# A hybrid mixer's tokens in a new order: convolution inputs first, retention gates made movable

## The chip, the cores and the metric

The kernel runs on one core of one Trainium2 chip. The metric is the device time of one call, in microseconds. Before the change the median of 3 runs is 2538.73 us (2537.46 to 2539.43).

## What is computed

One inference step of two trunk layers over 640 tokens of width 1024 (128 context tokens, 512 latent ones). Each layer is feed-forward, mixer, feed-forward, each added to x. The change touches the mixer alone. It projects the normed x by `w_in` into twelve pieces and runs four parallel head groups of width 256, which `w_out` brings back:

```python
aq, ak, av, bq, bk, bv, cx, cy, dq, dk, dv, dg = split_columns(u)
# A: windowed attention, normed q and k, 2-D rotary, cached context keys, a sink logit
oa = window_attention(axial_rope(qa), axial_rope(ka), va, kca, vca, sink)
# B: dense attention over cached context plus all latent tokens
ob = dense_attention(axial_rope(qb), concat([kcb, axial_rope(kb)]), concat([vcb, vb]), None)
# C: width-4 convolution, gates, recurrence h = a*h + b both ways, GeLU branch
xc = centred_conv(cx, conv_w, conv_b)
r, i = sigmoid(xc @ wa + ba), sigmoid(xc @ wx + bx)
a = exp(-8 * r * softplus(-lam));  b = sqrt(1 - a*a) * i * xc
oc = (hf + hb) * gelu(cy)
# D: retention both ways, normed per head, swish gate
o = rms_norm_per_head(retention(dq, dk, dv)) * gain
od = silu(dg) * o
x = x + g2 * (concat([oa, ob, oc, od]) @ w_out)
```

The context tokens run the same formulas among themselves, and their keys, values and final states are outputs too.

## The kernel before, in words

The kernel works on x transposed: 8 tiles of 128 features by 640 tokens. A product in fp32 is made of three passes over a high and a low part (`mm3`, lines 274 to 276): high by high, high by low, low by high. Weights arrive from memory as `raw` (512 KB each) and are split on chip: ScalarE writes `whi` (L169), VectorE writes `wlo` (L170).

The mixer is cut into **tokens**. Each stream is a generator, and one letter of the string `ORDER` lets that generator issue its next piece. So the string sets the program order on every engine, and with it the order in which the weight loads, the slots of the tile rings and the PSUM banks are asked for. A scheduler then moves instructions of different tokens past each other by priority; `order` rows below are the result. The streams are:

- `C` the branch of the convolution and its gates (`conv`, `gates`, `gelu_in`, lines 874 to 927), `L` the recurrence (`lru`, from L931: products on GpSimd, scans on VectorE at L961 to L966).
- `a`, `b` the projections dq and dk of the two head pairs of retention (`dproj`, from L982), `v` its values in natural layout, `r`, `s` retention itself (`retention`, from L1032). In it `rs` is the score product, `pm` the score times the decay mask `tt` on VectorE (L1068), and `ro` the product with the values (L1074). The end of `retention` multiplies by the gain and by the gate `sg` (L1136, L1137).
- `p`, `q` the projections q, k, v of the two attentions (`qkv`, from L1144): two passes of five blocks each. A block is 24 matmuls of 128x256 into `nat` (L1026 to L1028), then a chain through VectorE and GpSimd: sum of squares (L1191, L1192), power -1/2 on GpSimd (L1194), scale (L1196), gain on GpSimd (L1198), rotary on both (L1210, L1213), add (L1215 or L1224).
- `t`, `u` the transposes of finished q and k blocks on TensorE (`tr`, L1165), copied out at L1168, L1169, L1173 and L1174. They need the add of their blocks.
- `m`, `n` the scores of the windowed and dense attention (L1271, L1272) with row maximum (L1297), exponential (L1306) and scale (L1313); `M`, `N` the transposes of the probabilities (`pt` L1323, copied to `PT` at L1324) and the products with the values (`ao` L1332); `c` halves of the down projection (`dn`).
- `|` changes the PSUM pools from 3 two-bank score tiles and 2 one-bank tiles to 2 and 4, and `!` loads the cached keys and values (`load_cache`, L1243).

All wide tiles (split weights, masks `tt`, probabilities `P` and `PT`, cached keys) share one ring of slots, so a load waits until its slot's last reader is done. ScalarE, VectorE and GpSimd each run their list strictly in order.

The mixer opens with `first(l, 1)`, which projects three column chunks of `w_in` straight after the norm. They are the first three in the packed weight `wint`.

Of the kernel before, what the change touches and what calls it, by code (L numbers as in the profile page):

```python
# [4 lines left out]
F32 = mybir.dt.float32  # L5
F32R = mybir.dt.float32r
BF = mybir.dt.bfloat16
AF = mybir.ActivationFunctionType
OP = mybir.AluOpType
AX = mybir.AxisListType.X  # L10

L = 2
T = 640
# [25 lines left out]
SUM1 = 1  # L39
BC1 = 4  # L40
ORDER = (
    "CaCCCCvLvrLarvvvLLLbsLvpLrprbrssrqsrsrLsptrsLpppqLp|spqtpqLsptqpqpqtq!mqmmqMmqMmMmqMmMmuMmcMmuMmMmcM"
    "mMmuMmcMmuMmMmcMmMmcMnMnMMncNnNncNnNncNnNncNnNncNnNnNncNnNncNnNncNnNnNNcNcNc",) * L


def segs(a, b):
# [8 lines left out]
def trunk(tc, A, O):  # L55
    nc = tc.nc
    V, S, G, PE, D = nc.vector, nc.scalar, nc.gpsimd, nc.tensor, nc.sync
    from contextlib import ExitStack, nullcontext
    with ExitStack() as es:
# [24 lines left out]
        def slot(name, dt=F32, w=SLOT):  # L84
            return wp.tile([128, w], dt, tag="w", name=name)
# [150 lines left out]
        def plan():  # L236
            for l in range(L):
                ffn_units(l, 0)
                own = {"C": {0: 3, 1: 4, 3: 5}, "a": {0: 6, 1: 7}, "b": {0: 8, 1: 9}}
                own = {t: {i: [(A["wint"][l, c], 1024)] for i, c in v.items()} for t, v in own.items()}  # L240
                own["v"] = {0: [(A["wdv"][l, h], 1024) for h in range(2)]}
                for t, m in (("p", 0), ("q", 1)):
                    own[t] = {6 * i: [(A["wqkv"][l, m, 2 * i + h], 1024) for h in range(2)] for i in range(2)}
                own["c"] = {4 * h: [(A["wocd"][l, h], 1024)] for h in range(4)}
                for c in range(3):
                    plain(A["wint"][l, c], 1024)
                done = {}
# [482 lines left out]
        C = {}  # L730

        def mixer_consts():
# [14 lines left out]
            used = [0]  # L747

            def tiny(name, w):
                if name in ("lru_n", "lru_p", "lg", "nlg", "kdec", "dgain8"):  # L750
                    return cp.tile([128, w], F32, name=name)
                used[0] += w
                return temps[:, used[0] - w:used[0]]
# [77 lines left out]
            G.tensor_tensor(kdec, ebase[:, :8 * L], kd_x, op=OP.pow)  # L831

            dgain = ccol[:, 38 * L:40 * L]
            dgain8 = tiny("dgain8", 2 * L)
            V.tensor_scalar(dgain8, dgain, 8.0, None, OP.mult)
            C.update(rcos=rcos, rsin=rsin, masks=masks, idb=idb, blk2=blk2, ccol=ccol, sink=sink, negsink=negsink, stc=stc, lru_n=lru_n, lru_p=lru_p, lg=lg, nlg=nlg, kdec=kdec, dgain8=dgain8)

        def mixers(l):
            rcos, rsin, masks, idb, blk2, ccol, sink, negsink, stc, lru_n, lru_p, lg, nlg, kdec, dgain8 = [C[n] for n in "rcos rsin masks idb blk2 ccol sink negsink stc lru_n lru_p lg nlg kdec dgain8".split()]
            cc = ccol  # L840
            CW = lambda j, c: cc[:, l * 10 + c * 5 + j:l * 10 + c * 5 + j + 1]
            o1 = 10 * L
# [3 lines left out]
            o3 = 18 * L  # L846
            H0 = lambda d, c: cc[:, o3 + l * 4 + d * 2 + c:o3 + l * 4 + d * 2 + c + 1]
            o4 = 22 * L
            DG = lambda c: dgain8[:, l * 2 + c:l * 2 + c + 1]
            SN = lambda d, c: lru_n[:, l * 4 + d * 2 + c:l * 4 + d * 2 + c + 1]  # L850
            SPc = lambda d, c: lru_p[:, l * 4 + d * 2 + c:l * 4 + d * 2 + c + 1]

# [5 lines left out]


            other()  # L860
            h, (v0, v1, vcx), _ = first(l, 1)
            sg = []
            for v in (v0, v1):
                t = slot("sg", F32, T)
                S.activation(t, v, AF.Silu)
                sg.append(t)

            def tchunk(name):
                u = take()
# [8 lines left out]
            def conv(v, c):  # L878
                xp = slot("xp")
                G.memset(xp[:, 0:2], 0.0)  # L880
                G.memset(xp[:, 130:133], 0.0)
                G.memset(xp[:, 645:646], 0.0)
                S.activation(xp[:, 2:130], v[:, 0:128], AF.Copy)
                S.activation(xp[:, 133:645], v[:, 128:640], AF.Copy)
                y = slot("y")
                V.tensor_scalar(y[:, :643], xp[:, 2:645], CW(2, c), CW(4, c), OP.mult, OP.add)
                for j in (0, 1, 3):
                    V.scalar_tensor_tensor(y[:, :643], xp[:, j:j + 643], CW(j, c), y[:, :643], OP.mult, OP.add)
                ys.append(y)

            conv(vcx, 0)
            act = {}

            def gates(c):
# [19 lines left out]
                G.tensor_mul(x2, x2, cy)  # L914
                return x2, cy

            cys, gts = [], []

            def branch():
                conv(tchunk("cx"), 1)  # L920
                yield
                for c in range(2):
                    cys.append(gelu_in(tchunk("cy")))
                    yield
                    gts.append(gates(c))
                    yield

            def behind(name):
# [324 lines left out]

            def attention(m):
                qs, ks, vn = att[m]
                cv = cache["v"]
                for g in range(2):
                    if (2 * m + g) not in mixed:
                        mixed[2 * m + g] = (slot("mxh", F32R, T), slot("mxl", F32R, T))
# [6 lines left out]
                def scores(b, g, kv):  # L1266
                    q2 = qs[g][kv][:, b * 128:b * 128 + 128]

                    def mm2(out, keys, c, last=True):

                        PE.matmul(out, q2, keys[0][:, c], start=True, stop=False)  # L1271
                        PE.matmul(out, q2, keys[1][:, c], start=False, stop=last)  # L1272

                    p = psS("sc")
                    if b == 0:
                        mm2(p[:, 512:640], ks[kv], slice(0, 128))
                        lo, hi = 512, 640
                        vs = [vn[:, 0:128]]
                    else:
                        n = b - 1  # L1280
                        mm2(p[:, 256:512], cache["k"][kv], slice(m * 256, m * 256 + 256))
                        n0, n1 = (max(0, n - 1), min(4, n + 2)) if m == 0 else (0, 4)
                        w = (n1 - n0) * 128
                        k0 = 128 + n0 * 128
                        band = [(n - 1, 0), (n + 1, 1)] if m == 0 else []
                        band = [(j, i) for j, i in band if n0 <= j < n1]
                        mm2(p[:, 512:512 + w], ks[kv], slice(k0, k0 + w), not band)
                        for e, (j, i) in enumerate(band):
                            c0 = 512 + (j - n0) * 128
                            PE.matmul(p[:, c0:c0 + 128], idb, masks[:, i * 128:i * 128 + 128], start=False,  # L1290
                                      stop=e == len(band) - 1)
                        lo, hi = 256, 512 + w
                        vs = [cv[:, m * 256 + i * 128:m * 256 + i * 128 + 128] for i in range(2)]
                        vs += [vn[:, 128 + j * 128:256 + j * 128] for j in range(n0, n1)]
                    w = hi - lo
                    mx = small("mx", 1)
                    V.tensor_reduce(mx, p[:, lo:hi], AX, OP.max)  # L1297
                    nm = small("nm", 1)
                    if m == 0:
                        si = l * 4 + g * 2 + kv  # L1300
                        V.tensor_scalar(nm, mx, -0.125, negsink[:, si:si + 1], OP.mult, OP.min)
# [12 lines left out]
                    return P, w, vs
# [51 lines left out]
            def att_step(m, i):  # L1366

                if m not in attm:
# [2 lines left out]

            mod_until((l, 5))
            g2 = modt[(l, 5)]
            streams = {"C": branch(), "L": lru(), "a": dproj(0), "b": dproj(1), "v": dvalues(),
                       "r": retention(0), "s": retention(1), "p": qkv(0), "q": qkv(1), "t": qktr(0), "u": qktr(1),
                       "m": att_step(0, 0), "M": att_step(0, 1), "n": att_step(1, 0), "N": att_step(1, 1),
                       "c": down(KC, 2, 4, mixed, (4, 5, 6, 7), g2, halves=True)}
# [45 lines left out]
def _layout(inp):  # L1423
    import numpy as np
    f = np.float32
    a = {}
# [23 lines left out]
    def dn(w):  # L1450
# [3 lines left out]
    w = g["w_in"]  # L1454
    cw = cols(w)
    base = {"cx": 8, "cy": 10, "dq": 12, "dk": 14, "dv": 16, "dg": 18}
    order = [base["dg"], base["dg"] + 1, base["cx"], base["cx"] + 1, base["cy"], base["cy"] + 1,
             base["dq"], base["dk"], base["dq"] + 1, base["dk"] + 1]
    a["wint"] = asc(cw[:, order])

    def nat(cols_, kper):
# [94 lines left out]
```

## Time and profile before

| what | value |
|---|---|
| median of 3 runs | 2538.73 us (2537.46 to 2539.43) |
| the profiled execution's own time | 2538.78 us |
| its span in the trace | 2537.0 us |
| granted TensorE clock, mean | 0.985 |
| TensorE busy | 2448.2 us, 96% of the span |
| VectorE, ScalarE, GpSimd busy | 1986.8 us (78%), 1149.7 us (45%), 238.8 us (9%) |
| instructions | 43717 |

The profiled execution's time exceeds its span by 1.8 us, and it is within 0.1 us of the median, so microseconds read in the span can be taken off the time one for one. The mixer of layer 0 fills about 507 to 844 us, that of layer 1 starts 1247.0 us later (1753.98 us against 506.96 us for the first copy out of the opening chunks) and fills 1754 to 2092 us. The rest of the span is feed-forward and norms, which the diff does not touch.

### The profile page before, as it was taken

To read this page: it belongs to the slowest core of one execution; us is meant where nothing else is said; L and a number is where in the kernel's file an instruction comes from. 1 tells how busy PE (TensorE), PEld (TensorE's weight loads), DVE (VectorE), ACT (ScalarE), POOL (GpSimd) and SP (SyncE) were. 2 spreads that over 40 slices of the span, in tenths; PEclk is the share of its full clock that TensorE was granted. 3 is DMA by queue.
4 is the path that set the end of the run, shared out by engine and by line. 5 is a ranking of instruction groups with operands and counts; after the bars stand their busy time and mean duration, and the time that the engine had idled before them with its cause. 6 is when DMAs were issued, how large, how long until landed. Compare 5 with 4: busy or idle time off the path is not lost. (4 is left out here: it accounts for less than half of the span.)

```text
span 2537.0 us, 43717 instructions
## 1 busy us (share of the span) xinstructions
PE 2448.2 (96%) x17252; PEld 2363.3 (93%) x17252; DVE 1986.8 (78%) x3876; ACT 1149.7 (45%) x2301; POOL 238.8 (9%) x251
## 2 busy tenths in 40 slices
PE   7999999998889999999999999999997899999999
PEld 6999999996778999999999999999786799999999
DVE  5899989856576798988989898897656768666765
ACT  5344343563355634443463344344523646333433
POOL 2100000032500200000020000000433002000000
PEclk9999999999989999999999999999998999999999
DMA  7544334222002244443424444332110022222222
GB/s 252 190 151 142 124 132 140 88 82 70 17 26 67 85 152 139 142 128 121 142 88 147 133 142 133 125 125 78 59 58 22 18 76 80 72 74 77 91 79 72
DMA packets 92653, 262.39 MB, mean 103 GB/s; under 512 B 10144, under 2 KB 21024, under 8 KB 92448
## 3 DMA queue, kind: packets, MB, share of 16 engines
q1 hardware_dynamic: 92448, 259.60, 31.4%
q8 instruction: 136, 2.23, 0.4%
q14 instruction: 69, 0.57, 0.1%
HBM read 256.15 MB, written 3.41 MB: 102 GB/s over the span
## 5 line engine op out<-in xcount | busy, mean ns | idle before, releaser
L274 PE MATMUL dn<-hidh,wp 128*128 128x320 f32 x1408 | 434.3, 311 | 0.1
L275 PE MATMUL dn<-hidl,wp 128*128 128x320 f32 x1408 | 433.7, 309 | 0.2 <-DVE hidl L282 0.2
L276 PE MATMUL dn<-hidh,wp 128*128 128x320 f32 x1408 | 433.3, 309 | 0.0
L169 ACT ACTIVATE wp<-ws 128x512 fp32r<-128x512 f32 x288 | 180.6, 630 | 391.7 <-DVE ws L216 151.0
L683 DVE SCALAR_TENSOR_TENSOR x<-dn,mod,x 128x128 f32<-128x128 f32 (+3 forms) x488 | 234.3, 520 | 137.6 <-PE dn L276 136.6
L169 ACT ACTIVATE wp<-raw 128x512 fp32r<-128x512 f32 (+1 forms) x408 | 243.5, 611 | 208.9 <-DVE wp L170 84.2
L319 DVE SCALAR_TENSOR_TENSOR junk<-wm,cond 128x1024 bf16<-128x1024 f32 x256 | 305.0, 1221 | 5.3 <-DMA wm<-in_wmod 4.9
L170 DVE TENSOR_TENSOR wp<-raw,wp 128x512 fp32r<-128x512 f32 (+1 forms) x408 | 266.2, 668 | 51.8 <-ACT wp L169 47.3
L274 PEld LDWEIGHTS dn<-hidh,wp 128*128 128x128 f32 x1408 | 264.0, 188 | 4.6 <-ACT hidh L281 3.7
L275 PEld LDWEIGHTS dn<-hidl,wp 128*128 128x128 f32 x1408 | 264.4, 188 | 0.6 <-DVE hidl L282 0.6
L276 PEld LDWEIGHTS dn<-hidh,wp 128*128 128x128 f32 x1408 | 264.4, 188 | 0.0
L170 DVE TENSOR_TENSOR wp<-ws,wp 128x512 fp32r<-128x512 f32 x288 | 197.9, 692 | 17.3 <-ACT wp L169 16.8
L275 PE MATMUL g<-hl,whi 128*128 128x320 f32 x608 | 192.4, 317 | 2.1 <-DVE hl L529 1.4
L274 PE MATMUL g<-hh,whi 128*128 128x320 f32 x608 | 185.9, 318 | 4.6 <-ACT hh L528 1.9
L276 PE MATMUL g<-hh,wlo 128*128 128x320 f32 x608 | 190.3, 314 | 0.0
L274 PE MATMUL x<-hh,wp 128*128 128x320 f32 x576 | 178.2, 309 | 0.8 <-DVE sl L614 0.8
L276 PE MATMUL x<-hh,wp 128*128 128x320 f32 x576 | 178.2, 309 | 0.0
L275 PE MATMUL x<-hl,wp 128*128 128x320 f32 x576 | 178.0, 309 | 0.0
L170 DVE TENSOR_TENSOR wlo<-raw,whi 128x1024 fp32r<-128x1024 f32 x88 | 110.4, 1256 | 64.6 <-ACT whi L169 49.3
L426 POOL TENSOR_TENSOR nrs<-nrm,neghalf 80x4 f32<-80x4 f32 x12 | 13.3, 1107 | 1432.5 <-DVE nrm L424 1432.5
L1026 PE MATMUL nat<-whi,hh 128*128 128x256 f32 x400 | 119.5, 299 | 9.2 <-ACT qsq L1187 5.8
L169 ACT ACTIVATE whi<-raw 128x1024 fp32r<-128x1024 f32 x88 | 92.6, 1052 | 66.3 <-DVE pmc L1092 13.7
(333 smaller groups left out, 6646.2 us busy)
## 6 DMA issues: line engine op xcount, KB each, us to landing
raw<-in_wgu SPq DMA_DIRECT2D x176, 512.0 KB, 3.5
wm<-in_wmod SPq DMA_DIRECT2D x128, 512.0 KB, 3.6
raw<-in_wd SPq DMA_DIRECT2D x64, 512.0 KB, 3.9
raw<-in_wd SPq DMA_DIRECT2D x32, 384.0 KB, 3.3
raw<-in_wint SPq DMA_DIRECT2D x20, 512.0 KB, 3.5
wm<-in_wm SPq DMA_DIRECT2D x32, 256.0 KB, 6.2
raw<-in_wqkv SPq DMA_DIRECT2D x16, 512.0 KB, 3.4
raw<-in_wocd SPq DMA_DIRECT2D x8, 512.0 KB, 3.5
```

Of the source, the lines that this page charges most:

```text
L169: S.activation(hi, src, AF.Copy)
L170: V.tensor_sub(lo, src, hi.bitcast(F32))
L274: PE.matmul(out, wh, xh, start=first, stop=False, skip_group_check=more)
L275: PE.matmul(out, wh, xl, start=False, stop=False, skip_group_check=more)
L276: mark["pe"] = PE.matmul(out, wl, xh, start=False, stop=last, skip_group_check=more)
L319: V.scalar_tensor_tensor(junk, modraw["w"], 1.0, cond[c], OP.mult, OP.mult, accum_out=modraw[(l, g)][:, c, k:k + 1])
L426: G.tensor_tensor(r, s, neghalf[:80, :4], op=OP.pow)
L683: V.scalar_tensor_tensor(x[d][:, s0:s1], pv[:, s0 - base:s1 - base], gate[:, c, d:d + 1], x[d][:, s0:s1], OP.mult, OP.add)
L1026: PE.matmul(p[:, :n], hh[:, t0:t0 + 128], wh[:, w0:w0 + n], start=k == 0, stop=False)
```

## The change

The opening projects cx0, cx1 and cy0 in place of dg0, dg1 and cx0: the packed order of `wint` becomes cx0, cx1, cy0, cy1, dq0, dk0, dq1, dk1, dg0, dg1. Both convolutions and the first GeLU input are issued at once. Stream `C` is left with three tokens: gates of channel half 0, the second cy chunk, gates of half 1. The two dg chunks become a new stream `g` of two tokens, each a column chunk of 48 matmuls and the gate. The gate is written with tanh: silu(v) = 0.5 v (1 + tanh(v/2)), so ScalarE runs Tanh in place of Silu, VectorE adds one product, and the factor 0.5 goes into the gain constant (8.0 becomes 4.0). The string `ORDER` is new for the whole mixer; in it the cached keys and values are loaded after four more `q` tokens, and `cache["v"]` is looked up where it is read.

```diff
 ORDER = (
-    "CaCCCCvLvrLarvvvLLLbsLvpLrprbrssrqsrsrLsptrsLpppqLp|spqtpqLsptqpqpqtq!mqmmqMmqMmMmqMmMmuMmcMmuMmMmcM"
...
+    "CavLCCLrLvavsvrLvrLbgbLpvrrpsssrqsrsrLrptLLgsprppq|pLspqqtpsptppqqqq!mqtmqmqmMMmmqMMmMMMmuummMccummM"
...
-                own = {"C": {0: 3, 1: 4, 3: 5}, "a": {0: 6, 1: 7}, "b": {0: 8, 1: 9}}
+                own = {"C": {1: 3}, "a": {0: 4, 1: 5}, "b": {0: 6, 1: 7}, "g": {0: 8, 1: 9}}
...
-            dgain8 = tiny("dgain8", 2 * L)
-            V.tensor_scalar(dgain8, dgain, 8.0, None, OP.mult)
+            dgain4 = tiny("dgain4", 2 * L)
+            V.tensor_scalar(dgain4, dgain, 4.0, None, OP.mult)
...
-            h, (v0, v1, vcx), _ = first(l, 1)
+            h, firsts, _ = first(l, 1)
             sg = []
-            for v in (v0, v1):
-                t = slot("sg", F32, T)
-                S.activation(t, v, AF.Silu)
-                sg.append(t)
...
-            conv(vcx, 0)
+            for c in range(2):
+                conv(firsts[c], c)
...
-            cys, gts = [], []
+            cys, gts = [gelu_in(firsts[2])], []
 
             def branch():
-                conv(tchunk("cx"), 1)
+                gts.append(gates(0))
                 yield
-                for c in range(2):
-                    cys.append(gelu_in(tchunk("cy")))
-                    yield
-                    gts.append(gates(c))
+                cys.append(gelu_in(tchunk("cy")))
+                yield
+                gts.append(gates(1))
+                yield
+
+            def dgate():
+
+                for _ in range(2):
+                    v = tchunk("dg")
+                    t = slot("sg", F32, T)
+                    with behind("sqrt"):
+                        S.activation(t, v, AF.Tanh, scale=0.5)
+                    V.scalar_tensor_tensor(t, t, 1.0, v, OP.add, OP.mult)
+                    sg.append(t)
                     yield
...
-            streams = {"C": branch(), "L": lru(), "a": dproj(0), "b": dproj(1), "v": dvalues(),
+            streams = {"C": branch(), "L": lru(), "a": dproj(0), "g": dgate(), "b": dproj(1), "v": dvalues(),
```

What this moves is shown at three places of layer 0. The first is VectorE where the second head pair of retention is projected, ahead of the mask product `pm` of the scores on which the values' product `ro` waits. Before the change VectorE's list reads there (the rows with `ri` and `x_` are the recurrence):

```order
L966 SCALAR_TENSOR_TENSOR ri<-a,ccol,ri 128x512
L1045 TENSOR_TENSOR tt<-tt,idn 128x128
L968 COPY stc<-ri 128x1
L974 SCALAR_TENSOR_TENSOR x_5898<-x_5898,ri 128x128
L975 SCALAR_TENSOR_TENSOR x_5898<-x_5898,ri 128x512
L1045 TENSOR_TENSOR tt<-tt,idn 128x128
L170 TENSOR_TENSOR wlo<-raw,whi 128x1024
L282 TENSOR_TENSOR dql<-dq,dqh 128x640
L994 TENSOR_TENSOR ed<-ed,dq 128x512
L996 TENSOR_TENSOR qdb<-ed,dq 128x512
L1068 TENSOR_TENSOR pm<-rs,tt 128x512 x2
```

In the changed kernel, whose lines from there on are numbered 7 higher, the same place reads:

```order
L981 SCALAR_TENSOR_TENSOR x_5805<-x_5805,ri 128x128
L982 SCALAR_TENSOR_TENSOR x_5805<-x_5805,ri 128x512
L170 TENSOR_TENSOR wlo<-raw,whi 128x1024
L282 TENSOR_TENSOR dql<-dq,dqh 128x640
L1001 TENSOR_TENSOR ed<-ed,dq 128x512
L1003 TENSOR_TENSOR qdb<-ed,dq 128x512
L170 TENSOR_TENSOR wlo<-raw,whi 128x1024
L931 SCALAR_TENSOR_TENSOR sg<-sg,dg 128x640
L170 TENSOR_TENSOR wlo<-raw,whi 128x1024
L1009 SCALAR_TENSOR_TENSOR dkl<-dk,dkh 128x640
L1075 TENSOR_TENSOR pm<-rs,tt 128x512 x2
```

The recurrence has left this stretch, two weight splits, the new gate product and the dk split have come in ahead of the mask product, and two earlier `pm` pairs (one before the change) stand further up.

The second place is ScalarE at the end of the first attention's q blocks. It copies each block (`nat`) in the order in which TensorE makes them, and the transposed blocks (`tr`) out to `q2`. Block `nat_7258` is the last one that the transposes `tr_7311` need. Before the change:

```order
L1186 ACTIVATE q_7241<-nat_7215 128x128
L1187 ACTIVATE qsq_7240<-nat_7215 128x128
L1189 ACTIVATE vn_6489<-nat_7215 128x128
L169 ACTIVATE wp_7374<-ck_7371 128x512
L1186 ACTIVATE q_7284<-nat_7258 128x256
L1187 ACTIVATE qsq_7283<-nat_7258 128x256
L1173 ACTIVATE q2_7115<-tr_7311 64x512
L1173 ACTIVATE q2_7117<-tr_7320 64x512
L1186 ACTIVATE q_7355<-nat_7329 128x256
```

In the changed kernel the last block that the transposes `tr_7424` need is `nat_7174`, which stands ahead of these rows, with block 7215 between:

```order
L1193 ACTIVATE q_7284<-nat_7258 128x128
L1194 ACTIVATE qsq_7283<-nat_7258 128x128
L1196 ACTIVATE vn_6440<-nat_7258 128x128
L1193 ACTIVATE q_7339<-nat_7313 128x256
L1194 ACTIVATE qsq_7338<-nat_7313 128x256
L1312 ACTIVATE P_7374,sum_7375<-sc_7367,nm_7372 128x128
L1315 ACTIVATE esink_7377<-sink_1374,nm_7372 128x1
L1193 ACTIVATE q_7409<-nat_7383 128x256
L1194 ACTIVATE qsq_7408<-nat_7383 128x256
L1180 ACTIVATE q2_7117<-tr_7424 64x512
L1180 ACTIVATE q2_7119<-tr_7433 64x512
```

Four blocks of the second attention (7215, 7258, 7313, 7383) and a first score now stand between that block and the transposes, where before none did.

The third place is ScalarE early in the dense attention: `P` is the exponential of one score tile, `PT` copies transposed probabilities, `mxh` copies a finished output block. Before the change:

```order
L1306 ACTIVATE P,sum<-sc,nm 128x768
L1324 ACTIVATE PT<-pt 128x384 x2
L1306 ACTIVATE P,sum<-sc,nm 128x768
L1336 ACTIVATE mxh<-ao 128x128
L169 ACTIVATE whi<-raw 128x1024
L1324 ACTIVATE PT<-pt 128x384 x2
L1306 ACTIVATE P,sum<-sc,nm 128x768
L1324 ACTIVATE PT<-pt 128x384 x2
```

In the changed kernel:

```order
L1342 ACTIVATE mxh<-ao 128x128
L1312 ACTIVATE P,sum<-sc,nm 128x768
L1330 ACTIVATE PT<-pt 128x384 x2
L1342 ACTIVATE mxh<-ao 128x128
L1312 ACTIVATE P,sum<-sc,nm 128x768
L1330 ACTIVATE PT<-pt 128x384 x4
L1312 ACTIVATE P,sum<-sc,nm 128x768
L1342 ACTIVATE mxh<-ao 128x128
```

Where scores and probability transposes took turns, they now come in bunches of two and more (`PT` x4, and further on `P` x2).

## Rows read from the trace of the kernel before

**Rows 1.** Busy time by stretch, mixer of layer 0 (PEclk: granted TensorE clock).

```profile
core 0: us, PE busy (x) PEld busy (x) DVE busy (x) ACT busy (x) POOL busy (x), PEclk, DMA share, GB/s
582.00:592.00 10.00, 5.63 (x18) 3.65 (x17) 9.14 (x16) 1.47 (x2) 1.17 (x2) 0.66 0.06 21
615.00:652.00 37.00, 35.12 (x313) 33.70 (x312) 19.29 (x56) 12.43 (x39) 18.45 (x25) 1.00 0.16 49
667.00:684.00 17.00, 8.99 (x46) 8.55 (x45) 8.25 (x25) 3.74 (x9) 6.83 (x9) 0.70 0.00 1
698.00:730.00 32.00, 24.01 (x145) 19.71 (x144) 21.72 (x64) 16.73 (x49) 4.92 (x6) 0.73 0.11 34
730.00:760.00 30.00, 27.45 (x260) 23.86 (x258) 22.97 (x71) 20.62 (x65) 0.00 (x0) 1.00 0.06 19
760.00:844.00 84.00, 82.51 (x689) 76.47 (x688) 58.00 (x124) 47.41 (x100) 0.00 (x0) 1.00 0.21 69
sum 337.00, PE 306.69 PEld 271.82 DVE 216.64 ACT 165.45 POOL 74.84; mean PE 30.67 PEld 27.18 DVE 21.66 ACT 16.55 POOL 7.48
```

**Rows 2.** The same view of layer 1's mixer, two stretches and the sum.

```profile
1915.00:1932.00 17.00, 9.29 (x59) 8.85 (x58) 8.39 (x24) 3.86 (x9) 6.83 (x9) 0.83 0.01 2
1946.00:1978.00 32.00, 23.36 (x151) 19.16 (x152) 22.18 (x65) 16.62 (x49) 4.91 (x6) 0.79 0.10 33
sum 338.00, PE 307.77 PEld 273.24 DVE 218.32 ACT 163.14 POOL 75.13; mean PE 30.78 PEld 27.32 DVE 21.83 ACT 16.31 POOL 7.51
```

**Rows 3.** Waits of TensorE, 500 to 820 us: total us, times, longest.

```profile
PE tr L1165 <- DVE q L1215: 8.0, 2, 4.9
PE ro L1074 <- DVE pm L1068: 4.4, 1, 4.4
PE nat L1026 <- ACT qsq L1187: 2.9, 1, 2.9
PE nat L1026 <- DVE kd L1110: 1.7, 1, 1.7
```

**Rows 4.** Timeline of VectorE, 564 to 588 us (start, duration, engine, line).

```profile
582.64 1.21 DVE L170 TENSOR_TENSOR wlo<-raw,whi 128x1024 fp32r<-128x1024 f32 x1
585.70 1.28 DVE L1068 TENSOR_TENSOR pm<-rs,tt 128x512 f32<-128x512 f32 x2
```

**Rows 5.** Timeline of TensorE, 671 to 682 us.

```profile
672.27 1.11 PE L1165 MATMUL tr<-idn,q 128*128 128x128 f32 x4 [4.91 <-DVE q L1215]
...
677.16 0.28 PE L1027 MATMUL nat<-whi,hl 128*128 128x256 f32 x1
677.28 0.28 PE L1028 MATMUL nat<-wlo,hh 128*128 128x256 f32 x1
...
680.90 0.69 PE L1165 MATMUL tr<-idn,q 128*128 128x128 f32 x2 [3.10 <-DVE q L1215]
```

**Rows 6.** Timeline of GpSimd, 656 to 682 us, two powers.

```profile
667.71 1.01 POOL L1194 TENSOR_TENSOR qrr<-qss,neghalf 128x4 f32<-128x4 f32 x1 [1.07 <-DVE qss L1192]
...
676.67 1.01 POOL L1194 TENSOR_TENSOR qrr<-qss,neghalf 128x4 f32<-128x4 f32 x1 [1.68 <-DVE qss L1192]
```

**Rows 7.** Timeline of ScalarE at the opening, 506 to 522 us.

```profile
506.96 1.30 ACT L865 ACTIVATE sg<-g 128x640 f32<-128x640 f32 x2 [5.84 <-PE g L276]
508.14 0.28 ACT L883 ACTIVATE xp<-g 128x128 f32<-128x128 f32 x1
508.30 0.62 ACT L884 ACTIVATE xp<-g 128x512 f32<-128x512 f32 x1
...
515.72 1.06 ACT L169 ACTIVATE whi<-raw 128x1024 fp32r<-128x1024 f32 x1
516.80 1.28 ACT L991 ACT_TABLE_LOAD   x1
518.09 1.34 ACT L991 ACTIVATE ed<-t,lg 128x512 f32<-128x512 f32 x2
```

**Rows 8.** Groups by line and shape, layer 0's mixer (count, busy us, mean ns, idle before).

```profile
L888 DVE SCALAR_TENSOR_TENSOR y<-xp,ccol,y 128x643 f32<-128x643 f32 x6 | 5.3, 888 | 0.3
L940 ACT ACTIVATE ri<-ri,lru_p 128x643 f32<-128x643 f32 x4 | 3.3, 835 | 0.1
```

**Rows 9.** The page's DMA issues: count, KB each, median us to landing.

```profile
raw<-in_wint SPq DMA_DIRECT2D x20, 512.0 KB, 3.5
```

More of the change, by code (lines that the diff above doesn't have):

```diff
@@ L41 @@
 ORDER = (
-    "CaCCCCvLvrLarvvvLLLbsLvpLrprbrssrqsrsrLsptrsLpppqLp|spqtpqLsptqpqpqtq!mqmmqMmqMmMmqMmMmuMmcMmuMmMmcM"
-    "mMmuMmcMmuMmMmcMmMmcMnMnMMncNnNncNnNncNnNncNnNncNnNnNncNnNncNnNncNnNnNNcNcNc",) * L
+    "CavLCCLrLvavsvLrLvrLbgbLpvrrpsssrqsrsLrptLLgsprppq|pLspqqtpsptppqqqq!mqtmqmqmMMmmqMMmMMMmuummMccummM"
+    "mMmmcmMcMuMcmmMMmMMnnNmMncMnMNncnNNnMNnNcNncNnNnncNNnNcnNNncnnnNncNnNNNcccNN",) * L
 def segs(a, b):
@@ L749, in tiny @@
             def tiny(name, w):
-                if name in ("lru_n", "lru_p", "lg", "nlg", "kdec", "dgain8"):
+                if name in ("lru_n", "lru_p", "lg", "nlg", "kdec", "dgain4"):
                     return cp.tile([128, w], F32, name=name)
@@ L833, in mixer_consts @@
             dgain = ccol[:, 38 * L:40 * L]
-            dgain8 = tiny("dgain8", 2 * L)
-            V.tensor_scalar(dgain8, dgain, 8.0, None, OP.mult)
-            C.update(rcos=rcos, rsin=rsin, masks=masks, idb=idb, blk2=blk2, ccol=ccol, sink=sink, negsink=negsink, stc=stc, lru_n=lru_n, lru_p=lru_p, lg=lg, nlg=nlg, kdec=kdec, dgain8=dgain8)
+            dgain4 = tiny("dgain4", 2 * L)
+            V.tensor_scalar(dgain4, dgain, 4.0, None, OP.mult)
+            C.update(rcos=rcos, rsin=rsin, masks=masks, idb=idb, blk2=blk2, ccol=ccol, sink=sink, negsink=negsink, stc=stc, lru_n=lru_n, lru_p=lru_p, lg=lg, nlg=nlg, kdec=kdec, dgain4=dgain4)
         def mixers(l):
-            rcos, rsin, masks, idb, blk2, ccol, sink, negsink, stc, lru_n, lru_p, lg, nlg, kdec, dgain8 = [C[n] for n in "rcos rsin masks idb blk2 ccol sink negsink stc lru_n lru_p lg nlg kdec dgain8".split()]
+            rcos, rsin, masks, idb, blk2, ccol, sink, negsink, stc, lru_n, lru_p, lg, nlg, kdec, dgain4 = [C[n] for n in "rcos rsin masks idb blk2 ccol sink negsink stc lru_n lru_p lg nlg kdec dgain4".split()]
             cc = ccol
@@ L848, in mixers @@
             o4 = 22 * L
-            DG = lambda c: dgain8[:, l * 2 + c:l * 2 + c + 1]
+            DG = lambda c: dgain4[:, l * 2 + c:l * 2 + c + 1]
             SN = lambda d, c: lru_n[:, l * 4 + d * 2 + c:l * 4 + d * 2 + c + 1]
@@ L1255, in attention @@
                 qs, ks, vn = att[m]
-                cv = cache["v"]
                 for g in range(2):
@@ L1292, in scores @@
                         lo, hi = 256, 512 + w
-                        vs = [cv[:, m * 256 + i * 128:m * 256 + i * 128 + 128] for i in range(2)]
+                        vs = [cache["v"][:, m * 256 + i * 128:m * 256 + i * 128 + 128] for i in range(2)]
                         vs += [vn[:, 128 + j * 128:256 + j * 128] for j in range(n0, n1)]
@@ L1456, in _layout @@
     base = {"cx": 8, "cy": 10, "dq": 12, "dk": 14, "dv": 16, "dg": 18}
-    order = [base["dg"], base["dg"] + 1, base["cx"], base["cx"] + 1, base["cy"], base["cy"] + 1,
-             base["dq"], base["dk"], base["dq"] + 1, base["dk"] + 1]
+    order = [base["cx"], base["cx"] + 1, base["cy"], base["cy"] + 1,
+             base["dq"], base["dk"], base["dq"] + 1, base["dk"] + 1, base["dg"], base["dg"] + 1]
     a["wint"] = asc(cw[:, order])
```

## The prediction

> **What bounds the kernel now.** I began with the table: TensorE is busy for 96% of the span and VectorE for 78%, so only time in which TensorE stands, or runs at a low clock, can be won by another order. The diff touches only the mixers, so I went on to the busy time by stretch, as the stages have different limits. In [rows 1] the reader is to see two things for each stretch: length less PE busy, which is idle, and the granted clock. Layer 0's mixer has 337.00 - 306.69 = 30.3 us of idle, layer 1's 338.00 - 307.77 = 30.2 us [rows 2], in the same stretches. Where TensorE has stood, the granted clock falls between the two levels 1.2 and 2.4 GHz. I price that as PE busy times the missing share of clock, an estimate: 5.63 x 0.34 = 1.9 us in 582 to 592, 8.99 x 0.30 = 2.7 in 667 to 684, 24.01 x 0.27 = 6.5 in 698 to 730, 11.1 together. So about 41 us of a mixer can be won at the most, 83 in both, and the other 590 us of the two mixers is work that the change leaves as it is.
>
> Then I read the waits of TensorE [rows 3], to learn who ends each stretch. Three places hold nearly all of it:
> - 582 to 592, 4.4 us idle and 1.9 of clock: `ro` waits for `pm` on VectorE, which is 91% busy there [rows 1]. The mask product starts at 585.70, behind recurrence, a weight split and the dq products [rows 4].
> - 667 to 684, 8.0 idle and 2.7 of clock: the transposes of the first attention's q wait for its rotary add, 4.9 and 3.1 us [rows 3, 5]. The chain behind a block is slow, not TensorE: two blocks on, from 667.71 to 676.67, the power on GpSimd comes round again [rows 6], so a block takes 4.5 us of chain, against 24 matmuls 0.12 us apart [rows 5], 2.9 us of TensorE.
> - 698 to 730, 8.0 idle and 6.5 of clock: the windowed attention begins. 730 to 844 holds 2.55 + 1.49 more.
>
> **The change, part by part, for one mixer.** Matmuls are the same in number and size: the ten column chunks only change places, so TensorE's busy time at full clock stays.
>
> *Added and removed work.* Two Silu of 0.7 us (1.30 for both [rows 7]) go; two Tanh take their place, about 0.84 by the nearest row, and two products of VectorE come, 0.89 by the nearest [rows 8]. With the order a table load is added on ScalarE as well (six in a mixer, five before): 1.28 us [rows 7]. All this is 2 x 0.14 + 1.28 = 1.6 us on ScalarE and 1.8 on VectorE. ScalarE has 37 - 12.43 = 24.6 us free in 615 to 652, and VectorE 17.7 [rows 1], so I cost it at 0 there. Uncovered it would be 3.4 us; that is the upper end, and no reason speaks for a gain.
>
> The row of the load shows the next exponential starting at 518.09, 0.01 us after the load's end [rows 7]. The Trainium skill's "ScalarE: Activation LUTs", section "What ACT_TABLE_LOAD costs", speaks against one more switch: it gives 1283 ns for the load and about 1380 ns of drain, 2.66 us for each switch. By it, and with nothing covering the load, the two extra switches, one a mixer, would make the sum 5.3 us longer, 2520 us; the trace agrees with the 1283 ns and shows no drain behind it.
>
> *Opening.* The gates of half 0 now come as the first matmuls after the opening, and need copy, convolution and nothing else: 0.28 + 0.62 us of copies [rows 7] and four products of about 0.89 [rows 8], 4.5 us. The scheduler puts 39 value matmuls ahead of them, 39 x 0.12 = 4.7 us, but both convolutions share VectorE row by row, so the first ends up to 2.7 us later, three products. I add 1.2 us, between 0 and 4.5 (no cover at all).
>
> *Mask product.* The recurrence is through earlier, so `pm` no longer waits for scans. But three weight splits, the gate product and the dk split stand ahead of it in the new list, and the last split needs a weight that comes 3.5 us after its issue [rows 9], issued when a slot of the wide ring comes free. 6.3 us are lost at present. I leave 3.7 (about a landing), a gain of 2.6; bounds are a gain of 6.3 (all gone) and a loss of 3.5 (a second landing in a row).
>
> *Transposes of q.* Four blocks and a score now lie between the last needed block and its transposes, 4 x 2.9 = 11.5 us of cover against a stall of 4.9 and then 3.1. This is the term that carries the forecast. I leave 3.0 of 10.7 us, since the chain serves those four blocks too, and TensorE could meet it again at the next score; gain 7.7, bounds 10.7 and 0.
>
> *kd and first q block.* 1.7 + 2.9 us [rows 3]: the second dg chunk stands between the steps of retention's end, 48 matmuls of cover, which ends the first, and the second (ScalarE held behind a GpSimd product) may come back. Gain 2.3, bounds 4.6 and 0.
>
> *Attention.* 18.5 us are lost from 698 to 844 (14.5 + 2.55 + 1.49). Scores now run up to five ahead of the transposes in the windowed part, two before, which covers the softmax: I take a third of 14.5, 4.8. In the dense part the regular turns become bunches, with two score tiles in PSUM, where 2.55 + 1.49 are lost today: I add 4.0, which doubles that. Net a gain of 0.8; bounds a gain of 9 (half) and a loss of 8 (the dense part's loss tripled).
>
> *Later key cache* (4 loads behind the last weight): its keys are first needed by scores of later blocks, 0; the other edits issue nothing.
>
> Sum: 0 + 1.2 - 2.6 - 7.7 - 2.3 - 0.8 = -12.2 us a mixer, -24.4 for both, as layer 1 shows the same idle. The second layer's clock was higher in one stretch (0.83 against 0.70 [rows 1, 2]), worth 1 us, which I neglect. 2538.8 - 24.4 = 2514.4 for the execution profiled, and the same for the median, which is within 0.1 us of it: **2514 us**.
>
> **Rivals.**
> *A, the chain is the bound.* The blocks' chain takes 4.5 us of every block whatever the order, and the transposes' wait only moves to the next `nat` or score. For it speaks the period in [rows 6]; against it that other work of TensorE (retention's end, dg, scores) now lies among the blocks. Then the 7.7 us are not won: -4.5 a mixer, 2530 us.
> *B, the windowed attention is cured too.* With scores far ahead the stretch at clock 0.73 to 0.79 [rows 1, 2] keeps full clock. Attention then gains its 9: -12.2 - 8.2 = -20.4 a mixer, 2498 us. Against it: the exponentials and splits on ScalarE are as many as before.
> *C, slower: the dense part breaks.* Bunches "nnn" on two score tiles wait for the row maximum and exponential of the first, then the outputs come in bunches and the clock falls, as it does in 698 to 730 now. A second stretch like that one costs 14.5 us in place of the net gain of 0.8: -11.4 + 14.5 = +3.1 a mixer, 2545 us. It decides from 11.4 us of new loss on. Against it: 760 to 844 loses just 1.5 us now and has VectorE 69% and ScalarE 56% busy [rows 1], so there is slack.
> *D, nothing measurable*: gains and new waits cancel, 2534 to 2544.
>
> **How the numbers follow.** A time within 0.2% (5 us) is about what a measurement of this kernel can't tell from no change. Chances: the forecast 0.38, A 0.22, B 0.17, C 0.15, D 0.08. All of the first three are faster by over 0.2%, but a little of A's spread is not: faster 0.75, same 0.09, slower 0.16. The range holds the forecast, A, B's nearer part and D, and ends at 2541 below C: 2490 to 2541 leaves out about 2 in 10. The forecast's own range is 2504 to 2524: half the way to the bounds of mask and attention is about 2.5 and 4.3 us, which need not fall together, so some 5 us a mixer either way.
>
> **What would show it.** Right: the waits of `tr` on L1222 (the add) fall from 8.0 us to under 3 in each mixer, PE idle in the mixer from 30 to about 20, and no clock under 0.9 before the attention. A shows as `nat`, `sc` or `tr` waits of the same sum released by VectorE or GpSimd in the q blocks. B shows as a clock over 0.9 at the start of the windowed attention. C shows as `sc` and `pt` waits and a clock under 0.8 in the last 90 us of the mixer. The opening is wrong if the first `gate` waits over 3 us on VectorE, the mask term if `ro` waits over 5 us. What would make me wrong most easily is the dense part, on which no row of before bears directly, and the weights' arrival behind the reordered slots.

## The result and the profile after

The changed kernel takes 2506.18 us (median of 4 runs, 2503.04 to 2508.31) against 2538.46 us before: a ratio of 0.987 (95% interval 0.9855 to 0.9889), 32 us faster. The forecast was 2514 us. Sign and size held; the sum came out of other terms than the forecast had in it. One execution of the kernel with 17 thin tiles (below) took 11504.77 us at a granted clock of 0.194; it enters no figure here. (Two things on the change: the quoted diff lacks one L in the first line of the new order, as the program runs `CavLCCLrLvavsvLrLvrLbgb...`; and in both orders eight `q` tokens stand ahead of `!` and four behind it, so what moves past the load of the cached keys is the fourth `t`.)

The page of the changed kernel begins with busy time by engine:

```profile
span 2506.5 us, 43682 instructions
PE 2438.2 (97%) x17252; PEld 2350.6 (94%) x17252; DVE 1999.1 (80%) x3880; ACT 1153.0 (46%) x2303; POOL 248.4 (10%) x251
```

The span is 30.5 us shorter. The first copies out of the opening stand at 505.64 us in layer 0 and at 1737.33 in layer 1, 1231.7 us apart where it was 1247.0. So 15.3 us are won from one mixer to the next and 13.9 from the second to the end; 1.3 us come from ahead of the first opening, where the clock was 0.93 before and 1.00 after in 480 to 505 us, which the change doesn't touch.

To see where, layer 0's mixer is cut in both kernels at the same places of the program: the end of retention's products for the context tokens (`roc`), the last matmul of retention's norms (`rb`), the last q or k block (`nat`), the last transposes of the second attention (`tr`) and the last matmul of the down projection (`dn`). First the kernel before, in the view of busy time by stretch (PE, PEld, DVE, ACT, POOL busy, granted clock, DMA):

```profile
508.00:620.00 112.00, 107.49 (x693) 89.11 (x692) 70.43 (x101) 55.60 (x87) 31.57 (x22) 0.97 0.25 81
620.00:649.00 29.00, 27.15 (x239) 26.54 (x239) 16.10 (x48) 10.70 (x32) 15.51 (x21) 1.00 0.15 44
649.00:699.00 50.00, 37.99 (x280) 35.99 (x276) 27.27 (x91) 13.38 (x46) 23.11 (x31) 0.90 0.02 6
699.00:741.00 42.00, 33.21 (x231) 27.45 (x232) 29.38 (x87) 24.53 (x74) 4.65 (x6) 0.80 0.08 26
741.00:847.00 106.00, 102.85 (x873) 94.74 (x872) 74.55 (x176) 61.05 (x143) 1.00 (x1) 1.00 0.18 60
```

The same stages of the changed kernel:

```profile
506.00:612.00 106.00, 105.17 (x678) 87.05 (x676) 74.36 (x104) 55.49 (x87) 35.02 (x24) 1.00 0.25 81
612.00:640.00 28.00, 28.00 (x257) 27.38 (x257) 15.15 (x41) 11.63 (x33) 14.73 (x18) 1.00 0.21 65
640.00:694.00 54.00, 40.85 (x285) 38.44 (x282) 34.27 (x108) 16.12 (x55) 26.49 (x33) 0.84 0.02 6
694.00:726.00 32.00, 28.20 (x222) 23.49 (x222) 27.02 (x78) 21.09 (x64) 2.47 (x3) 0.95 0.12 37
726.00:831.00 105.00, 103.79 (x886) 93.98 (x883) 71.04 (x172) 61.54 (x146) 1.01 (x1) 1.00 0.18 60
```

The reader is to see two stages in which TensorE now hardly stands (106.00 - 105.17, and 28.00 of 28.00), a third that got worse (13.2 us idle at clock 0.84, where it was 12.0 at 0.90), and a fourth that lost most of its loss (3.8 us idle at 0.95, 8.8 at 0.80 before). What TensorE waits for in 500 to 830 us, against [rows 3]:

```profile
PE sc L1277 <- ACT P L1312: 6.4, 5, 5.2
PE nat L1033 <- ACT qsq L1194: 4.3, 2, 2.6
PE pt L1329 <- DVE P L1319: 2.3, 2, 1.6
PE nat L1033 <- DVE q L1181: 1.9, 1, 1.9
...
PE gate L898 <- DVE y L884: 0.3, 1, 0.3
...
PE ro L1081 <- DVE pm L1075: 0.2, 1, 0.2
```

`ro` went from 4.4 us to 0.2, and `tr`, 8.0 before, isn't in the list. But `nat` and `sc` have grown. The timeline of TensorE in 664 to 690 us shows these waits at the blocks of q:

```profile
666.60 1.04 PE L1172 MATMUL tr<-idn,q 128*128 128x128 f32 x8
667.39 0.31 PE L1277 MATMUL sc<-kkh,q 128*128 128x128 f32 x1
...
670.39 0.39 PE L1033 MATMUL nat<-whi,hh 128*128 128x256 f32 x1 [2.58 <-ACT qsq L1194]
...
683.48 0.48 PE L1277 MATMUL sc<-kkh,q 128*128 128x128 f32 x1 [5.20 <-ACT P L1312]
...
686.02 0.47 PE L1329 MATMUL pt<-idn,P 128*128 128x128 f32 x1 [1.61 <-DVE P L1319]
```

The transposes start without a wait now, as the forecast had it. But TensorE stands behind them instead, 2.6 us at the next block and 5.2 us at a score. That these are the 4.9 and 3.1 us moved on is what the run with the transposes early, below, is to show.

### The profile page after: what moved, and what is told of

Same layout as the page of the kernel before. It is cut to its first block, busy times and chain, and to the rows that moved or that the text cites. A ratio compares the mean times of both kernels' runs of the same rounds, so it can differ in the third digit from the quotient of the medians.

```text
span 2506.5 us, 43682 instructions
## 1 busy us (share of the span) xinstructions
PE 2438.2 (97%) x17252; PEld 2350.6 (94%) x17252; DVE 1999.1 (80%) x3880; ACT 1153.0 (46%) x2303; POOL 248.4 (10%) x251
## 5 line engine op out<-in xcount | busy, mean ns | idle before, releaser
L170 DVE TENSOR_TENSOR wp<-ws,wp 128x512 fp32r<-128x512 f32 x288 | 197.5, 691 | 17.3 <-ACT wp L169 16.7
L169 ACT ACTIVATE whi<-raw 128x1024 fp32r<-128x1024 f32 x88 | 92.6, 1052 | 65.7 <-DMA raw<-in_wqkv 18.9
```

The costliest lines, as they stand in the source:

```text
L169: S.activation(hi, src, AF.Copy)
L170: V.tensor_sub(lo, src, hi.bitcast(F32))
```

## The experiments

All times are medians, beside runs of the kernel before on the same chip (2538.3 to 2539.4 us there); a distance to the changed kernel is taken to its 2506.2 us. The ratio of each run has an interval of some 4 us to either side, so a distance of less than about 5 us is not told from none by the intervals alone. The loss of a stage is worked out the same way for each: idle of TensorE plus its busy time times the missing share of the granted clock, summed over slices of 2 us of the profiled run, layer 0, in us. The clock part is an estimate, good to some 2 us. Layer 1 repeats each entry within 2 us (before 7.8, 1.9, 15.6, 15.5, 3.2; changed 1.0, 0.0, 18.6, 6.6, 1.5).

| kernel | us | opening, retention | its end | q blocks | windowed | dense |
|---|---|---|---|---|---|---|
| before | 2538.5 | 7.1 | 1.9 | 15.7 | 16.2 | 3.2 |
| changed | 2506.2 | 0.8 | 0.0 | 20.1 | 5.3 | 1.2 |
| code alone | 2541.4 | 8.0 | 1.9 | 15.6 | 16.7 | 3.2 |
| new order to `\|` | 2525.5 | 0.8 | 0.0 | 18.0 | 15.8 | 3.2 |
| new order from `\|` | 2521.5 | 8.1 | 1.9 | 17.7 | 4.1 | 1.8 |
| old order from `!` | 2518.3 | 0.8 | 0.0 | 17.1 | 8.5 | 4.0 |
| dg first | 2517.5 | 4.5 | 1.1 | 18.9 | 4.0 | 1.5 |
| q transposes early | 2510.9 | 0.8 | 0.0 | 22.2 | 3.9 | 2.2 |
| 17 thin tiles | 2508.0 | 1.0 | 0.0 | 19.8 | 5.2 | 1.5 |
| products on VectorE | 2505.2 | 0.9 | 0.0 | 13.2 | 10.8 | 1.5 |
| both of these moves | 2509.5 | 0.8 | 0.0 | 15.6 | 10.4 | 2.2 |
| scores later | 2516.0 | 0.8 | 0.0 | 24.7 | 3.9 | 1.2 |
| chain cut short | 2475.2 | 0.9 | 0.0 | 4.6 | 3.7 | 1.5 |
| products on VectorE, chains overlapped | 2492.9 | 0.9 | 0.0 | 6.8 | 7.8 | 2.2 |

**Code alone.** The old order, rewritten for the new streams: the five `C` tokens become three and both `g` stand first.

From there on the string is that of before.

```diff
-    "CavLCCLrLvavsvLrLvrLbgbLpvrrpsssrqsrsLrptLLgsprppq|
+    "ggaCCCvLvrLarvvvLLLbsLvpLrprbrssrqsrsrLsptrsLpppqLp|
```

> The changed code (opening with cx0, cx1, cy0, tanh gates as a stream) under the order of before: both dg chunks stand at the very start, the convolution tokens that are gone are dropped, everything else in the old sequence. Theory 1, the order of the tokens carries the gain and the code by itself is neutral: 2538 us, within 4 us of before, ro still waits about 4 us for pm and tr about 8 us for the add. Theory 2, the earlier convolution inputs carry it: below 2530 us and the ro wait gone.

Ratio 1.001 (1.0000 to 1.0019). `ro` waits 4.5 us and `tr` 7.8, as before:

```profile
PE tr L1172 <- DVE q L1222: 7.8, 2, 4.9
PE ro L1081 <- DVE pm L1075: 4.5, 1, 4.5
```

Theory 1: the code carries nothing by itself, and the added ScalarE and VectorE work costs at most 0.2%. The two further table loads of the changed kernel are not in this run: its trace has 15 in a call, as before, and the changed kernel's 17. They come with the new order up to `|`; the next run has 17.

**New order up to the change of PSUM pools, and from it on.**

Two kernels, each with one half of the changed string. In the first, what follows `|` becomes that of before:

```diff
-|pLspqqtpsptppqqqq!mqtmqmqmMMmmqMMm
+|pspqtpqLsptqpqpqtq!mqmmqMmqMmMmqMm
```

In the second, what stands ahead of `|` becomes that of before, in the form of the run above:

```diff
-CavLCCLrLvavsvLrLvrLbgbLpvrrpsssrqsrsLrptLLgsprppq|p
+ggaCCCvLvrLarvvvLLLbsLvpLrprbrssrqsrsrLsptrsLpppqLp|
```

> The changed kernel with its order only up to the change of PSUM pools, the rest of the mixer in the order of before. Theory 1, losses by stage add up: retention's 6.3 us and the 1.8 us at its end are won, the q blocks' and windowed attention's losses of before come back, so 8 us a mixer below before, 2522 us. Theory 2, the first part's earlier end is what relieves the windowed attention: within 5 us of the changed kernel, 2506 us.

> The changed code with the old order up to the change of PSUM pools and the new one from there on. Theory 1, losses by stage add up: the q blocks lose 4 us more a mixer and the windowed attention 12 less, so 8 us a mixer below before, 2522 us, with ro still waiting about 4 us. Theory 2, the rest gains nothing without the first part: 2538 us.

Ratios 0.9942 (0.9927 to 0.9957) and 0.9927 (0.9912 to 0.9942): 13.9 and 17.9 us, together 31.8 of the 32 us: theory 1 in both, the two parts add up. The first half shows the old waits of the q transposes, the second the old wait of `ro`; first the new order up to `|`, then the new order from `|` on, in the view of TensorE's waits:

```profile
PE tr L1172 <- DVE q L1222: 7.3, 2, 3.7
```

```profile
PE ro L1081 <- DVE pm L1075: 4.5, 1, 4.5
```

**Old order from the key cache on.**

From `!` on the tokens are those of before, but for one `t`, to the end of the string (its second line is not shown).

```diff
-!mqtmqmqmMMmmqMMmMMMmuummMccummM
+!mqtmmqMmqMmMmqMmMmuMmcMmuMmMmcM
```

> The changed kernel with the old order only from the load of the cached keys on (the fourth q transposes put two tokens behind it). Theory 1, the lead of scores over probability transposes in the windowed attention is what gains there: its loss goes back from about 5.5 to about 17 us a mixer, 2506 + 24 = 2530 us. Theory 2, the q blocks being all issued before the attention is what gains: within 6 us of 2506 us. The forecast's fear, that bunches in the dense part cost 4 us a mixer, would show as up to 8 us won back against theory 1.

Ratio 0.9917 (0.9902 to 0.9931), 12 us above the changed kernel, in the middle between the two theories. About a third of what the windowed attention gains hangs on the order of its own tokens (its loss goes from 5.3 back to 8.5 us, where it was 16.2): with the old one the wait of `pt` for a copy that ScalarE holds back is there again, 3.2 us in the windowed part, 4.1 us in all of 693 to 836 us:

```profile
PE pt L1329 <- ACT PT L1330: 4.1, 2, 3.2
```

The rest comes with what stands between `|` and `!`, and that `t`: only there does this run differ from the new order up to `|`, whose windowed part loses 15.8 us against 8.5 here. That part in the run with the new order up to `|`, then in this one:

```profile
691.50:733.50 42.00, 32.98 (x233) 27.23 (x233) 29.51 (x88) 24.62 (x74) 4.81 (x6) 0.80 0.08 26
693.20:729.10 35.90, 28.89 (x235) 23.51 (x234) 27.63 (x84) 23.42 (x70) 3.19 (x4) 0.95 0.09 31
```

TensorE stands 2 us less, and the clock is 0.95 in place of 0.80. By what mechanism those tokens do it was not tested. And the bunched turns of the dense attention, which I feared, lose less than the old regular ones: 1.2 us against 4.0 here.

**dg first.** The two `g` go behind the first `C`.

```diff
-CavLCCLrLvavsvLrLvrLbgbLpvrrpsssrqsrsLrptLLgsprppq|
+CggavLCCLrLvavsvLrLvrLbbLpvrrpsssrqsrsLrptLLsprppq|
```

> The changed kernel with both dg chunks at the front of the mixer in place of in the middle of retention, all else in the new order. Theory 1, the movable dg chunks are what covers the mask product and the end of retention: ro waits 4 us or more again and the first nat behind kd about 1.7 us, 2506 + 12 = 2518 us. Theory 2, the recurrence's earlier place in the list is what frees VectorE: ro waits under 1 us, within 4 us of 2506 us.

Ratio 0.9925 (0.9908 to 0.9942), 11 us above the changed kernel by the medians and 7.2 by the profiled spans. `ro` waits 2.9 us, between the two theories. Both act: without dg as cover the wait is back by two thirds, and the recurrence's place accounts at most for the rest.

```profile
PE ro L1081 <- DVE pm L1075: 2.9, 1, 2.9
```

**q transposes early.** One token moves.

```diff
-ptppqqqq!mqtmqm
+ptppqtqqq!mqmqm
```

> The changed kernel with one token moved: the fourth transposes of the first attention's q stand one block behind the last block that they need, as before the change, in place of six tokens later. The prediction's step (four blocks and a score of cover win 7.7 us a mixer): the tr wait of about 8 us is back, 2506 + 15 = 2521 us. Rival A (the chain of the blocks is the bound and the wait only changes its place): the tr wait is back, the nat and sc waits of the same stretch shrink by as much, within 4 us of 2506 us.

Ratio 0.9892 (0.9877 to 0.9907), 4.8 us above the changed kernel. Within the q blocks (641 to 697 us) the waits read:

```profile
PE tr L1172 <- DVE q L1222: 6.4, 2, 3.8
PE sc L1277 <- ACT P L1312: 4.8, 2, 3.5
PE nat L1033 <- DVE q L1181: 1.9, 1, 1.9
PE nat L1033 <- ACT qsq L1194: 1.8, 1, 1.8
```

Sum 14.9 us, against 13.0 in the changed kernel (5.2 + 4.3 + 1.9 + 1.6 in 640 to 694). With the wait of `tr` back, others shrink: rival A, a little over its bound. The cover of four blocks is worth about 2.4 us a mixer, not 7.7; every execution of this run is above every one of the changed kernel (2510.57 us and more against 2508.31 and less), but the two intervals overlap, so the 2.4 is rough.

**17 thin tiles.**

```diff
-NSLOT = 41
-NTHIN = 14
+NSLOT = 40
+NTHIN = 17
```

> The changed kernel with 17 thin tiles in place of 14, paid for by one slot of the work ring (40 in place of 41). Theory 1, the late transposes hold thin tiles, so ScalarE can't copy the next block out and nat waits: the nat waits of about 6 us a mixer fall under 2, 2506 - 8 = 2498 us. Theory 2, the serial chain over VectorE and GpSimd sets the pace whatever the tiles: the waits move to the next reader, within 3 us of 2506 us.

Ratio 0.9879 (0.9863 to 0.9896), 1.8 us above the changed kernel. `nat` waits 2.3 us less for ScalarE (2.0 against 4.3), `sc` 2.2 us more (8.6 against 6.4):

```profile
PE sc L1277 <- ACT P L1312: 8.6, 6, 3.7
PE nat L1033 <- ACT qsq L1194: 2.0, 2, 1.7
```

Theory 2. Here the tiles decide where TensorE stands, not how long.

**Products on VectorE.**

```diff
-G.tensor_mul(q[:, :nw], q[:, :nw], gain[:, g0:g0 + nw])
+V.tensor_mul(q[:, :nw], q[:, :nw], gain[:, g0:g0 + nw])
-G.tensor_mul(q3, q3, cs)
+V.tensor_mul(q3, q3, cs)
```

> The changed kernel with the gain and the cosine product of each q, k block on VectorE in place of GpSimd: two crossings of engines a block fewer, VectorE 0.7 to 0.9 us a block busier. Theory 1, the serial chain of 4.5 us a block is the bound: it falls to about 3.3 us, the waits of nat, tr and sc among the blocks (about 13 us a mixer with 6 us of clock) fall by half, 2506 - 16 = 2490 us. Theory 2, VectorE itself becomes the bound or the tiles are: within 4 us of 2506 us or above it.

Ratio 0.9872 (0.9857 to 0.9887), 1.0 us below the changed kernel, no measurable change in all. The q blocks lose 6.9 us less, as theory 1 says, and the windowed attention 5.5 more. In all it is theory 2's number, by a cause that neither theory named. The last block is through 7 us earlier (686.3 us against 693.4) and its rotary add too (692.19 against 698.88), but behind it TensorE stands 2.5 us longer and runs at a lower clock. The first 12 us after the stage, here and in the changed kernel:

```profile
692.00:704.00 12.00, 10.25 (x64) 8.55 (x65) 7.61 (x24) 6.80 (x21) 0.00 (x0) 0.72 0.15 47
694.00:706.00 12.00, 10.58 (x88) 8.62 (x88) 10.49 (x32) 8.26 (x30) 2.47 (x3) 1.00 0.27 87
```

The granted clock is 0.72 there, where the changed kernel has 1.00. The products of the last blocks now stand on VectorE among the row maxima of the windowed scores; that these hold the scores up is argued from the list, not shown.

**Both of these moves together.** The two diffs above in one kernel.

> Gain and cosine products on VectorE together with the fourth q transposes one block behind their last block, as before the change. With those products on VectorE alone the q blocks lost 6 us less a mixer and the windowed attention 5 more; with the transposes alone the windowed attention lost 2 less and the q blocks 3 more. Theory 1, the two are independent: q blocks about 16, windowed attention about 4 a mixer, 2498 us. Theory 2, the loss only moves between the two stages because the same chain feeds both: within 4 us of 2506 us.

Ratio 0.9889 (0.9875 to 0.9904). Theory 2: the loss moves between the two stages (26.0 us in both together, 24.0 with the products alone and 25.4 in the changed kernel).

**Scores later.**

```diff
-!mqtmqmqmMMmmqMM
+!qtqqmmmmMMmmqMM
```

> The changed kernel with the first three windowed scores moved behind three more q blocks (the tokens after the key cache are q, transposes, q, q and then four scores). Theory 1, the row maximum of these scores stands on VectorE behind the norms of the q blocks, so the next scores wait for their tile: the sc wait of 5.2 us is gone and most of it shows at nat, since the chain stays, within 5 us of 2506 us. Theory 2, the early scores are a mistake of the new order: 2506 - 10 = 2496 us.

Ratio 0.9918 (0.9903 to 0.9933), 9.8 us above the changed kernel: both theories miss. The `sc` wait is not gone, it is one of 10.0 us:

```profile
PE sc L1277 <- ACT P L1312: 11.3, 5, 10.0
```

So early scores are no mistake of the new order, they are worth 5 us a mixer. Why a score waits at all is seen on VectorE in the changed kernel, 668 to 690 us (L1198 to L1222 belong to blocks but for L1181, which copies transposed q; L1303 is a score's row maximum), and on ScalarE:

```profile
678.16 0.43 DVE L1203 TENSOR_TENSOR q<-q,qrr 128x256 f32<-128x256 f32 x1 [0.41 <-POOL qrr L1201]
678.62 0.68 DVE L1181 TENSOR_TENSOR q<-tr,q 64x512 fp32r<-64x512 f32 x1
679.49 0.49 DVE L1217 TENSOR_TENSOR r<-q,rsin 128x128 f32<-128x128 f32 x2 [0.19 <-POOL q L1205]
...
682.07 0.29 DVE L1303 TENSOR_REDUCE mx<-sc 128x1 f32<-128x128 f32 x1
...
682.97 0.37 ACT L1312 ACTIVATE P<-sc,nm 128x128 f32<-128x128 f32 x1 [2.36 <-DVE nm L1307]
```

The score of 667.39 gets its row maximum at 682.07, 14.7 us later, behind the blocks' norms and rotary products and, from 677.07 on, four copies of transposed q of 0.7 us each. There are two score tiles, and the other one is taken from 674.65 on, so the score at 683.48 waits until the exponential behind that maximum, at 682.97, has read its tile.

**Chain cut short.** The gain on GpSimd, two sine products and the cosine product are left out for every q and k block; the time is read as that of a shorter chain.

```diff
-G.tensor_mul(q[:, :nw], q[:, :nw], gain[:, g0:g0 + nw])
...
-for a in range(2):
-    V.tensor_mul(r4[:, :, a::2, :], q4[:, :, 1 - a::2, :],
-                 sn[:, None, a::2, :].to_broadcast([128, nh, 2, 16]))
...
-G.tensor_mul(q3, q3, cs)
+r = q
```

> The changed kernel with the gain and the rotary products of every q and k block left out (gain on GpSimd, two sine products and the cosine product, with r taken as q), so the chain behind a block is sum of squares, power, scale and add. Theory 1, the length of that serial chain is what the first attention's blocks wait for, in either order: the loss of the q blocks falls from 19 us a mixer to under 6, 2506 - 27 = 2479 us. Theory 2, the copies out by ScalarE, the PSUM tiles or the score tiles are the bound: the loss stays over 13 us, above 2492 us.

Ratio 0.9753 (0.9739 to 0.9768), 31 us below the changed kernel. The matmuls are the same 17252, and the stage of the q blocks shrinks from 53 us to 37, in slices of the view of busy time by stretch:

```profile
640.00:680.00 40.00, 36.78 (x302) 35.40 (x299) 27.87 (x86) 16.55 (x57) 11.99 (x12) 0.96 0.03 8
```

Theory 1: it is the chain that these blocks wait for. The cut takes work off VectorE as well, but VectorE's load isn't the bound: with the two products moved to VectorE, which adds to its load, the q blocks lost 6.9 us less too.

**Products on VectorE, chains overlapped.** Beside that move, the loop over the blocks is cut in two, so that the second half of a block is written behind the first half of the next.

Here `norms` holds the copies, the sum of squares and the power, `turn` the scale, gain, rotary and add.

```diff
-for b in range(5):
+def norms(b):
     p = nat_block(us, b, 4, 256)
...
+    return q, rr
+
+def turn(b, q, rr):
...
+held = None
+for b in range(5):
+    now = norms(b)
+    if held:
+        turn(*held)
+    held = (b, *now)
+    if b in (0, 4):
+        turn(*held)
+        held = None
```

> The changed kernel with gain and cosine products on VectorE and with the second half of each block's chain (scale, gain, rotary, add) written behind the first half of the next block (sum of squares, power), so that VectorE has work while GpSimd computes the power. Theory 1, the serial chain is the bound: the q blocks lose under 10 us a mixer and the attention no more than with the products on VectorE alone, 2495 us. Theory 2, the scheduler already places these instructions by its own count and the written order matters little: within 4 us of 2505 us.

2492.9 us, ratio 0.9826 (0.9810 to 0.9843): theory 1, and 13 us faster than the changed kernel, with the whole computation done. The q blocks, then the windowed attention:

```profile
640.00:685.00 45.00, 40.63 (x323) 38.26 (x322) 36.97 (x124) 16.34 (x55) 12.45 (x12) 0.92 0.03 7
685.00:724.00 39.00, 32.65 (x262) 27.55 (x261) 32.30 (x94) 26.54 (x77) 1.01 (x1) 0.96 0.12 41
```

VectorE is 82% busy in the first of them (36.97 of 45.00), where it was 63% in the changed kernel. What the overlap does alone, with the products left on GpSimd, wasn't tried.

## Why the prediction was right, and where not

The bounding views held: nearly all that was won lies in idle and clock of the two mixers, and the matmuls are the same 17252. Of the sum:

- **Added work, 0**: right as far as it is seen. The code alone, without the added table loads, is at most 0.2% slower; with them the opening and retention of the changed kernel lose 0.8 us in all, so they are covered there.
- **Opening, +1.2**: too dear. The first `gate` waits 0.3 us.
- **Mask product, -2.6**: right in kind, the size was off: with the opening it gained 6.3 us (7.1 to 0.8). I left a weight's landing on the path, and `ro` waits 0.2 us. The dg chunks give most of it, as the run with dg first shows.
- **kd and first q block, -2.3**: the kd part is gone (1.9 to 0.0 at retention's end). The block held by ScalarE is not; `nat` waits for ScalarE 4.3 us now, 2.9 before.
- **Transposes of q, -7.7**: this is the step that failed. "Four blocks and a score now lie between" was true, and the wait of `tr` went as it said, but the stage of the blocks lost 4.4 us more than before. I counted the cover in TensorE's time, 11.5 us, and not what these blocks add to the same queue on VectorE and GpSimd. Rival A had the mechanism, by the period of 4.5 us a block [rows 6], and the cut chain shows it: with fewer links 15.5 of the 20.1 us are gone. Its sign came one step removed: of the 13.0 us of waits among these blocks ScalarE releases 9.5, but ScalarE had itself waited for VectorE (2.36 us ahead of the exponential at 682.97).
- **Attention, -0.8**: wrong in size. The windowed part went from 16.2 to 5.3 us, the dense one from 3.2 to 1.2, as rival B had it, with a clock of 0.95 where B wanted over 0.9. The cost of 4.0 for the bunches was not there. Where it comes from is shown in two parts: old tokens from the cache on lose 6 us more than the new ones in these two stages, and the tokens between `|` and `!` bring the windowed part from 15.8 to 8.5 us. By what mechanism the second part works stays open.

So two errors of 12.1 us a mixer each cancelled (+4.4 for -7.7, and -12.9 for -0.8): rival A's loss and rival B's gain came at once, and I had weighed them as alternatives. That the forecast came so near is luck in this part. What it fell short by, 8 us in all, is about what retention won beyond its two terms (-6.3 for -1.4 a mixer). Worked out with what was measured, -6.3 - 1.9 + 4.4 - 10.9 - 2.0 = -16.7 us by losses; the mixer itself became 14.8 us shorter from the first copy out of the opening to the last `dn` (340.3 to 325.5). Of that 11.3 is idle (30.3 to 19.0), so the clock gave back about 3.5 us, where the table's estimate has 5.4.

Of the signs I had named, two came (`tr` under 3 us, idle of a mixer at 325.0 - 306.0 = 19.0 us, forecast about 20) and one did not (no clock under 0.9 ahead of the attention: the blocks run at 0.84).

## What to carry to other kernels

Cover counted on the waiting engine is not enough. Where blocks feed a chain over other engines, ask for the chain's own period: if it is longer than a block takes on TensorE, moving the reader of its results mostly moves the wait (here 2.4 of the 7.7 us hoped for were won). A shorter chain or an overlapped one won time here; whether unrelated work among the blocks does was not tried. Then check what stands in the other engines' lists ahead of the next stage, as here norms and copies stood before the row maximum of a score.

## What the hardware showed that I had not expected

A chain that crosses between VectorE and GpSimd paid more for its work on GpSimd than for the crossings. In the changed kernel, power, scale and gain of one block read:

```profile
677.12 1.01 POOL L1201 TENSOR_TENSOR qrr<-qss,neghalf 128x4 f32<-128x4 f32 x1 [0.69 <-DVE qss L1199]
678.16 0.43 DVE L1203 TENSOR_TENSOR q<-q,qrr 128x256 f32<-128x256 f32 x1 [0.41 <-POOL qrr L1201]
678.73 0.73 POOL L1205 TENSOR_TENSOR q<-q,gain 128x256 f32<-128x256 f32 x1 [0.60 <-DVE q L1203]
```

From the end of one row to the start of the next are 0.03 us towards VectorE and 0.14 us towards GpSimd. By such rows, an estimate, the two products moved to VectorE (0.42 us each for 128x256 in place of 0.73) save 0.62 us of work and 0.34 us of four crossings a block. They took 6.9 us from a stage of 53 us, and yet gave 1.0 us in the end, until VectorE's list was rearranged with it. And dense attention on two score tiles didn't mind bunches of two and three scores: it lost 1.2 us, less than the 3.2 to 4.0 us with scores and transposes by turns.
